# Two fp32r parts of the activations in turn in one row, by stage, with displaced weights and three orders of the products

## The chip, the cores and the metric

The kernel runs on one core of one Trainium2 chip. The metric is the device time of one execution in microseconds. Two executions of the kernel before took 2337.79 and 2339.41 us; their median is 2338.6 us. The profile shown is of one further execution.

## The reference

The program is a two-layer decoder trunk over 272 tokens (16 learned prefix tokens and 256 inputs) of width 2048, with 16 heads of 128 and a squared-ReLU MLP of width 8192. Everything is float32. Layer 0 uses attention with a forget gate, layer 1 uses stick-breaking attention whose keys and values come from a separate projection of the stream:

```
for layer in range(DEPTH):                        # DEPTH = 2
    a = rms_norm(h, norm_attn[layer])
    if layer < N_A_LAYERS:
        proj = a @ fox_w_in[i]                    # q, k, v and the forget gate
        ...
        h = h + o.reshape(b, length, D_MODEL) @ fox_w_o[i]
    else:
        c = rms_norm(h, kv_norm)
        k_s, v_s = jnp.split(c @ w_kv, 2, axis=-1)
        q = split_heads(a @ sb_w_q[i])
        o = stick_breaking_attention(q, shared_k, shared_v)
        h = h + o.reshape(b, length, D_MODEL) @ sb_w_o[i]
    h = h + squared_relu_mlp(rms_norm(h, norm_mlp[layer]), w_up[layer], w_down[layer])
return rms_norm(h, final_norm)[:, N_META:]
```

## The kernel before

Activations lie feature-major: 128 features on the partitions, 16 chunks of features, and the tokens along the row. A matrix product of the model is made of groups (`gemm_group`). A group gives 512 output columns, as four PSUM accumulators (m = 0 to 3) of 128 columns each, over all 16 chunks of the contraction. There are 96 groups, numbered u = 1 to 96 in program order:

- 1 to 12: q, k, v of layer 0 from the activations `a0`, in turn with the attention;
- 13 to 16: output projection of layer 0, from `o0`;
- 17 to 48: MLP of layer 0, four rounds f of four "up" groups (from `m0`) and four "down" groups (from `u0_f`);
- 49 to 52: queries of layer 1 (from `a1`); 53 to 60: keys and values (from `kv`), in turn with the attention; 61 to 64: output projection (from `o1`);
- 65 to 96: MLP of layer 1, as before with `m1` and `u1_f`.

Layer 0, keys and values use all 272 tokens (t0 = 0); the rest of layer 1 uses 256 (t0 = 16).

Precision is kept by splitting. Every float32 operand is held as two fp32r parts: a rounded part, hi, which ScalarE (ACT) writes, and the rest, lo, which VectorE (DVE) writes by a subtraction. One chunk of one accumulator then takes three products with one pass each: weights hi with activations hi, weights hi with activations lo, and weights lo with activations hi. A group is 4 x 16 x 3 = 192 products, and the 96 groups are 18,432 (line L175). Each product carries its own load of 128 x 128 weights.

A weight block of two chunks is loaded by a DMA on SP's queue into a `raw` tile (4 buffers), split by ACT (L215, `whi`) and DVE (L216, `wlo`) into tiles of a pool of 4 buffers each, and used by 24 products. Each tile has rows of 576 elements, of which 512 are used, from element 0 on for 272 tokens and from element 16 on for 256.

The activations of a stage lie in a tile of class `Split`, 16 chunks at 640 elements each. Hi and lo are two contiguous stretches of that row: for 272 tokens at elements 48 and 368, for 256 tokens at elements 0 and 320. TensorE reads 272 or 256 elements in one piece for each product. `split_chunk`, `put_split` and the end of an up group in `mlp` write these parts.

The order of a group's products is fixed on TensorE by added dependencies (`gemm_matmul`). The three products of a chunk come one after the other for 272 tokens, and all products of one kind of a run come before the next kind for 256 tokens. The order of ACT's and DVE's work is set by a scheduler when the program is built.

Of the kernel before, what the change touches and what calls it, by code (L numbers as in the profile page):

```python
# [9 lines left out]
F32 = mybir.dt.float32  # L10
F32R = mybir.dt.float32r
AF = mybir.ActivationFunctionType
ALU = mybir.AluOpType
AX = mybir.AxisListType

P = 128
D = 2048
NC = D // P
M = 16
# [4 lines left out]
QSCALE = 1.0 / math.sqrt(P)  # L24
N_FF = 4

ROWS = {0: (48, 368), M: (0, 320)}
XROW = 640

G_A0, G_M0, G_KV, G_A1, G_M1, G_FIN = range(6)  # L30
# [3 lines left out]
def yoco_kernel(ctx: ExitStack, tc: tile.TileContext, hT_in, gains, b_f, w_f, w_qkv0, w_o0, w_up, w_dn,  # L34
                w_kv, w_q1, w_o1, outT):
    nc = tc.nc
# [5 lines left out]
    wspl = ctx.enter_context(tc.tile_pool(name="wspl", bufs=4))  # L42
# [9 lines left out]
    hT = const.tile([P, NC, T], F32, name="hT")  # L52
# [65 lines left out]
    class Split:  # L118


        def __init__(self, label, t0):
            n = T - t0
            self.t0 = t0
            rows = xs.tile([P, NC * XROW + 64], F32R, tag="x", name=f"x_{label}")
            hi, lo = ROWS[t0]
            rows = rows[:, hi:hi + NC * XROW].rearrange("p (c t) -> p c t", c=NC)
            d = lo - hi
            self.hi, self.lo = rows[:, :, :n], rows[:, :, d:d + n]

    def split_chunk(sp, gi, c):  # L130

        g = g_sb[:, gi, c:c + 1]
        nc.scalar.activation(sp.hi[:, c], hT[:, c, sp.t0:], AF.Copy, scale=g)
        nc.vector.scalar_tensor_tensor(out=sp.lo[:, c], in0=hT[:, c, sp.t0:], scalar=g,
                                       in1=sp.hi[:, c].bitcast(F32), op0=ALU.mult, op1=ALU.subtract)

    class Norm:

# [42 lines left out]
    def gemm_group(wblk, sp, t0, evac, before={}, after={}, load_x=None):  # L181

        uid[0] += 1
        u = uid[0]
        accs = [pacc.tile([P, 512], F32, tag="acc", name=f"acc_{u}_{m}") for m in range(4)]
        n = T - t0
        for kb in range(4):
            src_w = wblk[kb].rearrange("p (k c) -> p k c", k=4)  # L190
            if kb in before:
                before[kb]()
            piece = 1 if load_x is not None and kb < 2 else 2
            raws = [wraw.tile([P, 2, 512], F32, tag="raw", name=f"raw_{u}_{kb}_{hf}") for hf in range(2)]
            for k0 in range(0, 4, piece):
                if load_x is not None:
                    load_x(range(4 * kb + k0, 4 * kb + k0 + piece))
                if load_x is not None and kb == k0 == 0:

                    for c0 in (0, 256):  # L200
                        nc.scalar.dma_start(raws[0][:, 0, c0:c0 + 256], src_w[:, 0, c0:c0 + 256])
                else:
                    nc.sync.dma_start(raws[k0 // 2][:, k0 % 2:k0 % 2 + piece], src_w[:, k0:k0 + piece])
            parts = []
            for hf in range(2):
                whi, wlo = (wspl.tile([P, 2, 576], F32R, tag=f"w{x}", name=f"w{x}_{u}_{kb}_{hf}") for x in ("hi", "lo"))
                o = 16 if t0 else 0
                whi, wlo = whi[:, :, o:o + 512], wlo[:, :, o:o + 512]
                boxes = [(o, piece, 0, 512) for o in range(0, 2, piece)]
                if load_x is not None and kb == hf == 0:  # L210
                    boxes[:1] = [(0, 1, 0, 256), (0, 1, 256, 512)]
                for o, no, c0, c1 in boxes:
                    src = raws[hf][:, o:o + no, c0:c1]
                    hp, lp = whi[:, o:o + no, c0:c1], wlo[:, o:o + no, c0:c1]
                    on_act = nc.scalar.activation(hp, src, AF.Copy)  # L215
                    on_dve = nc.vector.tensor_tensor(out=lp, in0=src, in1=hp.bitcast(F32), op=ALU.subtract)  # L216
                parts.append((whi, wlo))
            if kb in after:
                with tc.issue_after(on_act.ins), tc.issue_after(on_dve.ins):
                    after[kb]()  # L220

            if load_x is not None and kb == 0:
                runs = [([kc], range(4)) for kc in range(4)]
            elif kb in (0, 3):
                runs = [(range(4), [m]) for m in range(4)]
            else:
                runs = [(range(2 * hf, 2 * hf + 2), range(4)) for hf in range(2)]
            pinned[0] = load_x is None
            for kcs, ms in runs:
                pairs = ((0, sp.hi), (0, sp.lo), (1, sp.hi))  # L230
                if t0:
                    products = [(kc, m, *pair) for pair in pairs for kc in kcs for m in ms]
                else:
                    products = [(kc, m, *pair) for m in ms for kc in kcs for pair in pairs]
                left = {m: 3 * len(kcs) for m in ms}
                for kc, m, part, x in products:
                    first, left[m] = kb == kc == 0 and left[m] == 3 * len(kcs), left[m] - 1
                    gemm_matmul(accs[m][:, :n], parts[kc // 2][part][:, kc % 2, m * P:(m + 1) * P], x[:, 4 * kb + kc],
                                start=first, stop=kb == kc == 3 and left[m] == 0)
                if kb == 3:  # L240
                    for m in ms:
                        evac(m, accs[m][:, :n])

    def residual_add(c, acc, t0):
        nc.vector.tensor_tensor(out=hT[:, c, t0:], in0=acc, in1=hT[:, c, t0:], op=ALU.add)  # L245
# [91 lines left out]
        return t  # L337

    def put_split(sp, h, nh, t, n, src):
        hi, lo = (x[:, h:h + nh, t - sp.t0:t - sp.t0 + n] for x in (sp.hi, sp.lo))  # L340
        nc.scalar.activation(hi, src, AF.Copy)
        nc.vector.tensor_tensor(out=lo, in0=src, in1=hi.bitcast(F32), op=ALU.subtract)

    ao = Split("o0", 0)
    for g in range(4):
# [37 lines left out]
        for j in range(4):  # L383
            h = 4 * g + j
# [4 lines left out]
            for i, (o, n) in enumerate(((0, 144), (144, T))):  # L389
                nc.vector.tensor_tensor_reduce(out=s[:, j, o:o + n], in0=ps[:, o:o + n], in1=s[:, j, o:o + n],  # L390
                                               scale=1.0, scalar=3.0e38, op0=ALU.add, op1=ALU.min,
# [4 lines left out]
            for i, (o, n) in enumerate(((0, 144), (144, T))):  # L396
# [7 lines left out]
                                       scalar=fqm_sb[:, g:g + 1], in1=maskM, op0=ALU.subtract, op1=ALU.add)  # L404
        nc.vector.tensor_tensor_reduce(out=s0, in0=ps[:64, :P], in1=s0, scale=1.0,
                                       scalar=3.0e38, op0=ALU.add, op1=ALU.min, accum_out=st[:64, 0:1])
# [6 lines left out]
        for pr in range(2):  # L413
            pp_sb = att.tile([P, 2, 416], F32, tag="pp", bufs=3, name=f"pp_sb_{g}_{pr}")
            for i in range(2):
# [14 lines left out]
                                in0=pm[:, P - M:P].unsqueeze(1).to_broadcast([P, 8, M]))  # L430
# [37 lines left out]
    def mlp(layer, xm, norm, t0, last_evac):  # L468
        box = {}

        def get_rstd():
            box["r"] = norm.finish()

        for f in range(N_FF):
            u = Split(f"u{layer}_{f}", t0)
            for g in range(4):
                def evac(m, acc, g=g):
                    c = 4 * g + m
                    r = tmp.tile([P, T], F32, tag="relu", name=f"relu_{layer}_{f}_{c}")
                    u2 = tmp.tile([P, T], F32, tag="u2", name=f"u2_{layer}_{f}_{c}")  # L480
                    nc.vector.scalar_tensor_tensor(out=r[:, t0:], in0=acc, scalar=0.0, in1=box["r"][:, t0:],
                                                   op0=ALU.max, op1=ALU.mult)
                    nc.scalar.activation(u2[:, t0:], r[:, t0:], AF.Square)
                    nc.scalar.activation(u.hi[:, c], u2[:, t0:], AF.Copy)
                    nc.vector.tensor_tensor(out=u.lo[:, c], in0=u2[:, t0:], in1=u.hi[:, c].bitcast(F32),
                                            op=ALU.subtract)
                gemm_group(w_up[layer, f, g], xm, t0, evac, {2: get_rstd} if f == g == 0 else {})
            for g in range(4):
                def evac(m, acc, g=g):
                    residual_add(4 * g + m, acc, t0)  # L490
                    if f == N_FF - 1:
                        last_evac(4 * g + m)
                gemm_group(w_dn[layer, f, g], u, t0, evac)
# [33 lines left out]
    for g in range(4):  # L527
# [30 lines left out]
        for pr in range(2):  # L558
# [3 lines left out]
            for i in range(2):  # L562
# [4 lines left out]
                                    in1=maskB[:, 0:256].unsqueeze(1).to_broadcast([P, 2, 256]))  # L567
            nc.vector.tensor_tensor(out=zp[:, :, 256:400], in0=pb[:, :, :144], op=ALU.add,
                                    in1=maskB[:, 256:400].unsqueeze(1).to_broadcast([P, 2, 144]))
# [15 lines left out]
            for t in (240, 384):  # L585
                nc.vector.tensor_tensor(out=zp[:, :, t:t + M], in0=zp[:, :, t:t + M],
                                        in1=sc[:, 2 * pr:2 * pr + 2, :], op=ALU.add)
# [47 lines left out]
    a, y, t, rs = (fin[:, i, :] for i in range(4))  # L635
# [18 lines left out]
    for c, n in [(12, 1), (13, 1), (14, 1), (15, 1), (0, 2), (2, 2), (4, 2), (6, 2)]:  # L654
        if n == 1:
            nc.vector.scalar_tensor_tensor(out=ob[:, c, :S], in0=hT[:, c, M:], scalar=g_sb[:, G_FIN, c:c + 1],
                                           in1=prs[0], op0=ALU.mult, op1=ALU.mult)
        else:
            nc.vector.tensor_tensor(out=ob[:, c:c + n, :S], in0=hT[:, c:c + n, M:], op=ALU.mult,  # L659
                                    in1=prs[0].unsqueeze(1).to_broadcast([P, n, S]))  # L660
        nc.sync.dma_start(outT[:, c:c + n, :], ob[:, c:c + n, :S])
    for c in (8, 10):
        nc.gpsimd.tensor_tensor(out=ob[:, c:c + 2, :S], in0=hT[:, c:c + 2, M:], op=ALU.mult,
                                in1=pr_sb.unsqueeze(1).to_broadcast([P, 2, S]))
# [52 lines left out]
```

## Time and profile before

| | before |
|---|---|
| median of two executions | 2338.6 us |
| profiled execution | 2337.68 us, span of its instructions 2335.9 us |
| TensorE, matmuls | 2325.1 us busy (100%), 19,030 instructions |
| TensorE, weight loads | 2312.5 us busy (99%) |
| DVE / ACT | 1291.4 us (55%) / 1041.1 us (45%) |
| DMA | 412.32 MB, mean 177 GB/s |
| granted TensorE clock | 0.998 |

Matmuls are pipelined: each lasts some 280 ns in the trace while the next starts after some 120 ns, so 100% busy does not say that TensorE works at its peak. What counts is the pace, the time from the start of one product to the start of the next. It comes out of a window of the trace: its length divided by the number of products in it.

### The profile page before, as it was taken

To read this page: it belongs to the slowest core of one execution; us is meant where nothing else is said; L and a number is where in the kernel's file an instruction comes from. 1 tells how busy PE (TensorE), PEld (TensorE's weight loads), DVE (VectorE), ACT (ScalarE), POOL (GpSimd) and SP (SyncE) were. 2 spreads that over 40 slices of the span, in tenths; PEclk is the share of its full clock that TensorE was granted. 3 is DMA by queue.
4 is the path that set the end of the run, shared out by engine and by line. 5 is a ranking of instruction groups with operands and counts; after the bars stand their busy time and mean duration, and the time that the engine had idled before them with its cause. 6 is when DMAs were issued, how large, how long until landed. Compare 5 with 4: busy or idle time off the path is not lost.

```text
span 2335.9 us, 44808 instructions
## 1 busy us (share of the span) xinstructions
PE 2325.1 (100%) x19030; PEld 2312.5 (99%) x19030; DVE 1291.4 (55%) x1764; ACT 1041.1 (45%) x1397; POOL 39.7 (2%) x58
## 2 busy tenths in 40 slices
PE   9999999999999999999999999999999999999998
PEld 9999999999999999999999999999999999999998
DVE  7666556554455455455665555566555555555554
ACT  6434345443343344344444444445434444443553
POOL 1000000000000000000000000000000000000000
PEclk9999999999999999999999999999999999999999
DMA  7544545555555555555555444455565655656553
GB/s 237 167 160 158 181 154 164 185 177 179 180 171 184 172 186 175 181 173 185 171 190 184 156 145 147 148 184 192 180 193 177 198 183 179 197 182 191 180 190 127
DMA packets 116648, 412.32 MB, mean 177 GB/s; under 512 B 13264, under 2 KB 16736, under 8 KB 116448
## 3 DMA queue, kind: packets, MB, share of 16 engines
q1 hardware_dynamic: 114560, 406.29, 53.6%
q8 instruction: 149, 2.44, 0.5%
q10 hardware_dynamic: 1888, 3.16, 0.4%
q14 instruction: 51, 0.42, 0.1%
HBM read 407.29 MB, written 2.11 MB: 175 GB/s over the span
## 4 chain that ended last, share of the span: by engine, by line
PE 99%; DMA 1%; DVE 0%; ACT 0%; issue 0%; SPq 0%; DVEq 0%; ACTq 0%
PE acc L175 95%; DMA hT<-hT_in 1%; PE ps L387 0%; PE pza L564 0%; PE pv L320 0%; PE po L449 0%; PE po L603 0%; PE po L604 0%; PE pzb L565 0%; PE po L450 0%; PE po L605 0%; DVE ob L659 0%; PE pf L287 0%; PE pf L286 0%; PE pta L579 0%; PE pta L580 0%
## 5 line engine op out<-in xcount | busy, mean ns | idle before, releaser
L216 DVE TENSOR_TENSOR wlo<-raw,whi 128x1024 fp32r<-128x1024 f32 (+1 forms) x773 | 928.1, 1217 | 770.7 <-ACT whi L215 769.3
L215 ACT ACTIVATE whi<-raw 128x1024 fp32r<-128x1024 f32 (+1 forms) x773 | 795.8, 1049 | 1023.6 <-PE acc L175 1003.1
L175 PE MATMUL acc<-x_u,whi 128*128 128x272 f32 (+1 forms) x4096 | 651.9, 284 | 0.0
L175 PE MATMUL acc<-x_m,whi 128*128 128x272 f32 (+1 forms) x4096 | 651.7, 284 | 0.0
L175 PEld LDWEIGHTS acc<-x_m,whi 128*128 128x128 f32 x4096 | 573.7, 189 | 0.1
L175 PEld LDWEIGHTS acc<-x_u,whi 128*128 128x128 f32 x4096 | 573.8, 189 | 0.0
L175 PE MATMUL acc<-x_u,wlo 128*128 128x272 f32 (+1 forms) x2048 | 445.3, 284 | 0.0
L175 PE MATMUL acc<-x_m,wlo 128*128 128x272 f32 (+1 forms) x2048 | 445.2, 284 | 0.0
L175 PE MATMUL acc<-x_a,whi 128*128 128x272 f32 (+1 forms) x2048 | 362.2, 289 | 0.1
L175 PEld LDWEIGHTS acc<-x_u,wlo 128*128 128x128 f32 x2048 | 327.6, 189 | 0.0
L175 PEld LDWEIGHTS acc<-x_m,wlo 128*128 128x128 f32 x2048 | 327.5, 189 | 0.0
L175 PEld LDWEIGHTS acc<-x_a,whi 128*128 128x128 f32 x2048 | 303.7, 189 | 2.1 <-issue 0.7
L175 PE MATMUL acc<-x_a,wlo 128*128 128x272 f32 (+1 forms) x1024 | 255.0, 287 | 0.0
L175 PE MATMUL acc<-x_kv,whi 128*128 128x272 f32 x1024 | 194.1, 288 | 0.0
L175 PEld LDWEIGHTS acc<-x_a,wlo 128*128 128x128 f32 x1024 | 176.7, 189 | 0.9 <-issue 0.5
L175 PE MATMUL acc<-x_o,whi 128*128 128x272 f32 (+1 forms) x1024 | 162.2, 282 | 0.0
L175 PEld LDWEIGHTS acc<-x_kv,whi 128*128 128x128 f32 x1024 | 160.6, 188 | 0.4
L175 PE MATMUL acc<-x_kv,wlo 128*128 128x272 f32 x512 | 147.3, 288 | 0.0
L175 PEld LDWEIGHTS acc<-x_o,whi 128*128 128x128 f32 x1024 | 141.9, 188 | 0.1
L245 DVE TENSOR_TENSOR hT<-acc,hT 128x272 f32<-128x272 f32 (+1 forms) x160 | 69.1, 432 | 88.1 <-PE acc L175 86.8
L175 PE MATMUL acc<-x_o,wlo 128*128 128x272 f32 (+1 forms) x512 | 110.5, 282 | 0.0
L175 PEld LDWEIGHTS acc<-x_kv,wlo 128*128 128x128 f32 x512 | 96.5, 188 | 0.1
(221 smaller groups left out, 972.2 us busy)
## 6 DMA issues: line engine op xcount, KB each, us to landing
raw<-w_up SPq DMA_DIRECT2D x256, 512.0 KB, 4.4
raw<-w_dn SPq DMA_DIRECT2D x256, 512.0 KB, 4.4
raw<-w_qkv SPq DMA_DIRECT2D x92, 512.0 KB, 3.8
raw<-w_o SPq DMA_DIRECT2D x64, 512.0 KB, 4.1
raw<-w_kv SPq DMA_DIRECT2D x64, 512.0 KB, 3.8
raw<-w_q SPq DMA_DIRECT2D x32, 512.0 KB, 4.6
fk<-f_dram ACTq DMA_DIRECT2D x4, 544.0 KB, 5.2
raw<-w_qkv SPq DMA_DIRECT2D x7, 256.0 KB, 4.4
```

Source lines behind the costliest of these rows:

```text
L175: ins = nc.tensor.matmul(*args, **kw).ins
L215: on_act = nc.scalar.activation(hp, src, AF.Copy)
L216: on_dve = nc.vector.tensor_tensor(out=lp, in0=src, in1=hp.bitcast(F32), op=ALU.subtract)
L245: nc.vector.tensor_tensor(out=hT[:, c, t0:], in0=acc, in1=hT[:, c, t0:], op=ALU.add)
```

## The change

The same products are computed. Changed are where the parts lie and, in some stages, the order of the products.

Activations: a table by stage says how hi and lo share a row. A unit of 0 keeps two stretches (`a0`, `kv`, `u0_1`, at elements 48 and 368 as before). Any other unit puts hi and lo in turn, in pieces of that many elements: 16 (64 bytes) for `o0`, `m0`, `u0_0`, `u0_3`, `a1` and `m1`; 8 (32 bytes) for `u0_2` and `u1_3`; 32 for `o1` and `u1_0`; 64 for `u1_1`; 128 (512 bytes) for `u1_2`. A product then reads its part in pieces of one unit with gaps of one unit. ACT and DVE write the parts in the same pieces.

Weights: hi and lo of a block share one tile of rows of 1088 elements, hi in 512 elements and lo in the next 512, starting at element o. Function `way(u)` gives o, by the group's place g = 0 to 3 in its stage: 0 for groups 1 to 12 and 53 to 60, 16g (64 bytes a step) elsewhere, and in the down groups of layer 1 16 times g // 2. In the up groups of round f = 3 of both layers the elements of hi and lo alternate, so that a weight load steps by two elements.

Order of the products: ABC (the three of a chunk in turn), BAC (weights hi with activations lo first) or SERIES (kind by kind). Up groups use ABC, BAC, SERIES, ABC in rounds f = 0 to 3. Down groups of layer 1 alternate ABC and SERIES. All others use ABC; so `a1` and `o1` go from SERIES to ABC.

```
+ROWS = {"a0": (0, 48), "kv": (0, 48), "o0": (16, 0), "m0": (16, 0), "u0_0": (16, 0), "u0_1": (0, 48), "u0_2": (8, 0),
+        "u0_3": (16, 0), "a1": (16, 0), "o1": (32, 0), "m1": (16, 0), "u1_0": (32, 0), "u1_1": (64, 0),
+        "u1_2": (128, 0), "u1_3": (8, 0)}
+ABC, BAC, SERIES = range(3)
+def way(u):
+    if u <= 12 or 53 <= u <= 60:
+        return 0, 0, ABC
+    f, g = divmod((u - 17) % 48, 8) if 17 <= u <= 48 or u >= 65 else (0, (u - 1) % 4)
+    if 5 <= u <= 16 or u in (49, 50, 51, 52, 61, 62, 63, 64):
+        return 0, 16 * g, ABC
+    if g < 4:
+        return f == 3, 16 * g, (ABC, BAC, SERIES, ABC)[f]
+    g -= 4
+    if u < 49:
+        return 0, 16 * g, ABC
+    return 0, 16 * (g // 2), (ABC, SERIES)[g % 2]
...
-            hi, lo = ROWS[t0]
-            rows = rows[:, hi:hi + NC * XROW].rearrange("p (c t) -> p c t", c=NC)
-            d = lo - hi
-            self.hi, self.lo = rows[:, :, :n], rows[:, :, d:d + n]
+            self.unit, o = ROWS[label]
+            rows = rows[:, o:o + NC * XROW].rearrange("p (c t) -> p c t", c=NC)
+            if self.unit:
+                rows = rows[:, :, :2 * n].rearrange("p c (l i t) -> p c l i t", i=2, t=self.unit)
+                self.hi, self.lo = rows[:, :, :, 0], rows[:, :, :, 1]
+            else:
+                self.unit = 16
+                self.hi, self.lo = lines(rows[:, :, :n], 16), lines(rows[:, :, 320:320 + n], 16)
...
-                whi, wlo = (wspl.tile([P, 2, 576], F32R, tag=f"w{x}", name=f"w{x}_{u}_{kb}_{hf}") for x in ("hi", "lo"))
-                o = 16 if t0 else 0
-                whi, wlo = whi[:, :, o:o + 512], wlo[:, :, o:o + 512]
+                apart, o, order = way(u)
+                both = wspl.tile([P, 2, 1088], F32R, tag="w", name=f"w_{u}_{kb}_{hf}")[:, :, o:o + 1024]
+                if apart:
+                    both = both.rearrange("p k (t i) -> p k i t", i=2)
+                    whi, wlo = both[:, :, 0], both[:, :, 1]
+                else:
+                    whi, wlo = both[:, :, :512], both[:, :, 512:]
...
-                if t0:
+                if order == BAC:
+                    pairs = pairs[1], pairs[0], pairs[2]
+                if order == SERIES:
                     products = [(kc, m, *pair) for pair in pairs for kc in kcs for m in ms]
```

`split_chunk`, `put_split` and the end of an up group in `mlp` read and write the same numbers of elements as before, through views cut into pieces of a unit (`lines`).

More of the change, by code (lines that the diff above doesn't have):

```diff
@@ L25, with lines @@
 N_FF = 4
-ROWS = {0: (48, 368), M: (0, 320)}
+ROWS = {"a0": (0, 48), "kv": (0, 48), "o0": (16, 0), "m0": (16, 0), "u0_0": (16, 0), "u0_1": (0, 48), "u0_2": (8, 0),
[14 more added lines that the diff above has]
+    return 0, 16 * (g // 2), (ABC, SERIES)[g % 2]
+def lines(x, unit):
+    return x.rearrange("p c (l t) -> p c l t", t=unit)
 XROW = 640
@@ L124, in __init__ @@
             rows = xs.tile([P, NC * XROW + 64], F32R, tag="x", name=f"x_{label}")
-            hi, lo = ROWS[t0]
-            rows = rows[:, hi:hi + NC * XROW].rearrange("p (c t) -> p c t", c=NC)
-            d = lo - hi
-            self.hi, self.lo = rows[:, :, :n], rows[:, :, d:d + n]
+            self.unit, o = ROWS[label]
[6 more added lines that the diff above has]
+                self.hi, self.lo = lines(rows[:, :, :n], 16), lines(rows[:, :, 320:320 + n], 16)
     def split_chunk(sp, gi, c):
         g = g_sb[:, gi, c:c + 1]
-        nc.scalar.activation(sp.hi[:, c], hT[:, c, sp.t0:], AF.Copy, scale=g)
-        nc.vector.scalar_tensor_tensor(out=sp.lo[:, c], in0=hT[:, c, sp.t0:], scalar=g,
-                                       in1=sp.hi[:, c].bitcast(F32), op0=ALU.mult, op1=ALU.subtract)
+        src = lines(hT[:, c:c + 1, sp.t0:], sp.unit)
+        nc.scalar.activation(sp.hi[:, c:c + 1], src, AF.Copy, scale=g)
+        nc.vector.scalar_tensor_tensor(out=sp.lo[:, c:c + 1], in0=src, scalar=g,
+                                       in1=sp.hi[:, c:c + 1].bitcast(F32), op0=ALU.mult, op1=ALU.subtract)
     class Norm:
@@ L339, in put_split @@
     def put_split(sp, h, nh, t, n, src):
-        hi, lo = (x[:, h:h + nh, t - sp.t0:t - sp.t0 + n] for x in (sp.hi, sp.lo))
+        l0 = (t - sp.t0) // sp.unit
+        hi, lo = (x[:, h:h + nh, l0:l0 + n // sp.unit] for x in (sp.hi, sp.lo))
+        src = lines(src, sp.unit)
         nc.scalar.activation(hi, src, AF.Copy)
@@ L483, in evac @@
                     nc.scalar.activation(u2[:, t0:], r[:, t0:], AF.Square)
-                    nc.scalar.activation(u.hi[:, c], u2[:, t0:], AF.Copy)
-                    nc.vector.tensor_tensor(out=u.lo[:, c], in0=u2[:, t0:], in1=u.hi[:, c].bitcast(F32),
+                    src = u2[:, t0:].rearrange("p (c l t) -> p c l t", c=1, t=u.unit)
+                    nc.scalar.activation(u.hi[:, c:c + 1], src, AF.Copy)
+                    nc.vector.tensor_tensor(out=u.lo[:, c:c + 1], in0=src, in1=u.hi[:, c:c + 1].bitcast(F32),
                                             op=ALU.subtract)
```

## The prediction

> **What bounds the kernel now.** I read the page first, then TensorE's waits, then windows of the stages.
>
> ```profile
> span 2335.9 us, 44808 instructions
> ...
> PE 2325.1 (100%) x19030; PEld 2312.5 (99%) x19030; DVE 1291.4 (55%) x1764; ACT 1041.1 (45%) x1397; POOL 39.7 (2%) x58
> ...
> PE 99%; DMA 1%; DVE 0%; ACT 0%; issue 0%; SPq 0%; DVEq 0%; ACTq 0%
> PE acc L175 95%; DMA hT<-hT_in 1%; PE ps L387 0%; PE pza L564 0%; PE pv L320 0%; PE po L449 0%; PE po L603 0%; PE po L604 0%; PE pzb L565 0%; PE po L450 0%; PE po L605 0%; DVE ob L659 0%; PE pf L287 0%; PE pf L286 0%; PE pta L579 0%; PE pta L580 0%
> ```
>
> The chain that ended last is TensorE for 99%, the products of line L175 for 95%. Its waits, in us in total, times, longest:
>
> ```profile
> PE pr_fin L648 <- DVE fin L642: 1.3, 1, 1.3
> PE idle L61 <- DVE mean_w L57: 1.1, 1, 1.1
> PE pms_fin L616 <- ACT sq_fin L628: 0.3, 1, 0.3
> ```
>
> That is 2.7 us in all, so only the pace of 18,432 products counts. One ns on each is 18.4 us, and a change of 2% (some 47 us, about what a measurement of this kernel can tell from no change) is 2.5 ns. Windows: the MLP of layer 0 without its first 20 ns, the last three groups of `o1`, and 30 groups of the MLP of layer 1; the count includes two or three products open at the edges.
>
> ```profile
> 429.80:1187.90 758.10, 758.10 (x6148) 758.02 (x6147) 396.83 (x484) 326.81 (x419) 0.00 (x0) 1.00 0.55 178
> 1532.80:1598.00 65.20, 65.20 (x578) 65.20 (x577) 42.55 (x60) 33.89 (x49) 0.00 (x0) 1.00 0.61 194
> 1620.80:2299.20 678.40, 678.40 (x5762) 678.40 (x5761) 363.96 (x432) 302.55 (x385) 0.00 (x0) 1.00 0.58 187
> ```
>
> These hold 32, 3 and 30 groups of 192 products, so the paces are 758.1/6144 = 123.4 ns at 272 tokens and 65.2/576 = 113.2 or 678.4/5760 = 117.8 ns at 256 tokens. The last two differ though code, form and layout are the same. Within one group of `m1`, before and after the two matmuls of the norm that interrupt it, it flips:
>
> ```profile
> 1598.10:1608.90 10.80, 10.80 (x98) 1.00 0.52 158
> 1609.80:1620.60 10.80, 10.80 (x94) 1.00 0.65 213
> ```
>
> Less some 2.5 open at the edges that is 113 and 118 ns. Both stretches use the same addresses modulo 256 bytes. So at 256 tokens there are two stable phases of weight loads against rows, 4.6 ns apart, and a break chooses between them.
>
> How far is that from the stream itself? Mean ns of one by form:
>
> ```profile
> L175 PE MATMUL acc<-x_m,whi 128*128 128x272 f32 x2048 | 379.3, 287 | 0.0
> L175 PE MATMUL acc<-x_m,whi 128*128 128x256 f32 x2048 | 272.4, 281 | 0.0
> L387 PE MATMUL ps<-kT,qT 128*128 128x272 f32 x32 | 9.9, 393 | 0.0
> L387 PE MATMUL ps<-kT,qT 128*128 128x144 f32 x32 | 6.5, 285 | 0.0
> L286 PE MATMUL pf<-x_a,wf 128*32 128x272 f32 x16 | 4.1, 286 | 0.0
> L579 PE MATMUL pta<-eh,ntri_r 128*128 128x512 f32 x8 | 3.2, 395 | 0.0
> L581 PE MATMUL pta<-eh,nones_r 128*128 128x288 f32 x8 | 2.4, 296 | 0.0
> ```
>
> Plain float32 matmuls (L387) take (393 - 285)/128 = 0.84 ns a column. An fp32r product at 272 takes about half a float32 one's share, so I put its stream at 0.42 ns a column: 114 ns for 272, 107 for 256. Above the stream stand 9.7 ns at 272, and 6.2 or 10.8 ns at 256. The gate products (L286) load only 32 columns of weights and last as long as the others, 286 against 287 ns: the excess at 272 hangs on reading the row.
>
> **The change part by part.** The profiled execution took 2337.7 us, 1.8 beyond its span and 0.9 under the median. I sum against 2337.7.
>
> *Unchanged.* Groups 1 to 12, 53 to 60 and group 29 (`u0_1`, g = 0) keep layout, displacement modulo 256 bytes and order: 21 of 96, no cost. Transfers keep sizes and queues.
>
> *Units of 16 and 8.* At 272 tokens these are 32 groups (6144 products): `o0` 4, `m0` 16, `u0_0`, `u0_2`, `u0_3` 4 each. At 256 they are 24 groups (4608): `a1` 4, `m1` 16, `u1_3` 4. No row shows fp32r rows read in such small pieces. The nearest are L579 and L581, two pieces each. From 272 to 288 columns the stream explains 6.7 of 296 - 287 = 9 ns, leaving 2.3 ns for one break, if all of it is the break's. From 272 to 512 it explains 101 of 108 ns, leaving 7 ns for 240 columns and one break; in proportion, the excess of 272 alone would be 9.7 x 240/272 = 8.6 ns, leaving nothing for the break. So a break costs 0 to 2.3 ns. I take nothing for the break itself, by the longer row, but let the excess grow with the stretch of row that is walked. A half-used stretch doubles the 128-byte pieces touched: 8.5 more at 272, 8 more at 256. The excess per piece is 6.2/8 = 0.8 to 10.8/8 = 1.35 ns. I take 0.8, since part of the excess will belong to each product, not to its length. That is 6.8 ns x 6144 = 42 us and 6.4 ns x 4608 = 29 us. The lower end is below nothing, as a new phase can gain (second rival).
>
> [...]
>
> *Units of 32, 64 and 128* (`o1`, `u1_0`, `u1_1`, `u1_2`, 16 groups): whole 128-byte pieces, as many as before: 0. At 2.3 ns a break (7, 3 and 1) it would be 16, 7 and 2 ns a product.
>
> *Displacement.* Before, every pair of weights and row starts 64 bytes apart modulo 256. Now 53 groups differ (10,176 products). The size of a changed meeting of the two streams is the flip's 4.6 ns, either way: 47 us up or down at most. As interleaved rows meet several displacements at once, I take 0.
>
> *Orders.* 192 products and 192 loads a group remain, and the flip happens within one order. I take 0, inside the same bound.
>
> *Alternating weights* (8 groups, 1536 products).
>
> ```profile
> L175 PEld LDWEIGHTS acc<-x_m,whi 128*128 128x128 f32 x4096 | 573.7, 189 | 0.1
> L286 PEld LDWEIGHTS pf<-x_a,wf 128*32 128x32 f32 x16 | 1.7, 108 | 0.2
> ```
>
> A load takes (189 - 108)/96 = 0.84 ns a column, 108 ns for 128. It is hidden under a pace of 118 to 123 ns, with 10 to 15 ns to spare. A step of two elements costs nothing while it fits there. If the load takes twice as long, the pace becomes 216 plus the 5 ns that separate 108 from 113.2, thus 221: 768 x (221 - 123.4) + 768 x (221 - 117.8) = 154 us. I take 0, because rows already pass through at twice a load's bytes per ns.
>
> *ACT and DVE.* They write the same elements, in pieces.
>
> ```profile
> L216 DVE TENSOR_TENSOR wlo<-raw,whi 128x1024 fp32r<-128x1024 f32 x764 | 922.3, 1224 | 769.9 <-ACT whi L215 768.5
> L215 ACT ACTIVATE whi<-raw 128x1024 fp32r<-128x1024 f32 x764 | 790.6, 1055 | 1021.5 <-PE acc L175 1003.1 <-ACT sq_m L150 6.4 <-DMA fqm_sb<-f_dram 5.1
> ```
>
> Eight blocks a group cost DVE 9.8 and ACT 8.4 us of a group's 22.6 to 23.7; TensorE covers them. Doubled, DVE's 52% in the first window becomes 94%, still under. Hi and lo in one tile mean that ACT's next hi part waits for the last reader of lo as well. In SERIES that is 8 products, 0.9 us; the block is due three blocks (72 products, 8.5 us) later and takes 1.06 + 1.22 us. With that cover gone each late block would stall TensorE by its excess. I take 0.
>
> Sum: 2337.7 + 42 + 29 = 2409 us.
>
> **The rivals.**
>
> *The layout does not matter.* For it: paces are constant over thousands of products while ACT, DVE and DMA work beside them, and the 512-column row shows no break. Against it: the flip. The phases at 256 may settle otherwise; all 36 slow groups at 113.2 would give 36 x 192 x 4.6 = 32 us less. So 2338, between 2305 and 2365.
>
> *Faster.* The interleaved row takes weights and rows apart at the start of each product. The groups at 256 then stay at 113.2 (32 us less), and half of the 9.7 ns goes in the 35 changed groups at 272: 6720 x 4.85 = 33 us. That is 2273. It decides once the products at 272 gain 2.3 ns besides all groups at 256. For it: the flip shows 4.6 ns to be had with the same code. Against it: at 272 no second pace appears in 6144 products. [...]
>
> *Far slower.* Either each break costs 2.3 ns: 16 breaks a product at 272 and unit 16 are 37 ns, over all stages 2.3 x (5376 x 16 + 768 x 33 + 3840 x 15 + 1536 x 7 + 768 x 35) = 475 us, 2813 us. Or alternating weights double the load: 2409 + 154 = 2563 us. For it: L581. Against it: L579.
>
> **How the numbers follow.** Forecast 0.43, its own range 2365 to 2465 (0.5 to 1.35 ns a piece and part of the displacement). No effect 0.29, faster 0.14, far slower 0.14. The range 2275 to 2565 leaves out about half of each outer rival. Slower by over 2% are the far slower rival and nearly all of the forecast, 0.54; within 2% the first rival and the forecast's lower end, 0.32; faster 0.14.
>
> **What would show it.** Right: in windows, groups 17 to 24 and 41 to 48 near 130 ns and the first rounds of `m1` near 120 to 124; `u1_1` and `u1_2` within 113 to 118; group 29 at 123.4. The weight load of round 3 longer than 189 ns, but its pace no worse than that of round 0. Wrong: one pace for all units (first rival), paces under 120 at 272 (second), a pace that falls with 8, 16, 32, 64, 128 as the breaks do, or 221 ns in round 3 (third). A wait of TensorE for ACT or DVE of over 10 us in all would break the cover that I assume.

## The result, and the profile after

The changed kernel takes 2389.36 us (2389.03 and 2389.70) against 2338.6 us: a ratio of 1.022, 95% interval 1.0203 to 1.0237, slower by 50.8 us. The forecast was slower, 2409 us, with 2275 to 2565.

The page of the changed kernel, the same parts as before:

```profile
span 2387.2 us, 44824 instructions
...
PE 2376.2 (100%) x19030; PEld 2364.0 (99%) x19030; DVE 1289.7 (54%) x1764; ACT 1042.4 (44%) x1397; POOL 35.7 (1%) x58
...
PE 99%; DVE 0%; ACT 0%; issue 0%; DVEq 0%; ACTq 0%
```

TensorE's waits are the three of before, 2.7 us in all:

```profile
PE pr_fin L689 <- DVE fin L683: 1.3, 1, 1.3
PE idle L88 <- DVE mean_w L84: 1.1, 1, 1.1
PE pms_fin L657 <- ACT sq_fin L669: 0.3, 1, 0.3
```

So nothing new is waited for, and the granted clock is 0.998 as before. The span grew by 51.3 us and TensorE's busy time by 51.1: the products follow each other more slowly. Windows of the changed kernel, each of whole groups: `u0_0`, group 29, `u0_2`, the last three of `o1`, the up groups of round 1 in layer 1, `u1_1` in two halves, and three groups of `u1_3`:

```profile
532.49:631.27 98.78, 98.78 (x770) 1.00 0.51 171
729.84:754.16 24.32, 24.32 (x195) 1.00 0.53 174
924.47:1021.06 96.59, 96.59 (x770) 1.00 0.53 175
1566.40:1635.73 69.33, 69.33 (x578) 1.00 0.55 183
1820.80:1913.41 92.61, 92.61 (x770) 1.00 0.55 183
1913.41:1959.48 46.07, 46.07 (x386) 1.00 0.57 183
1959.48:2004.71 45.23, 45.23 (x386) 1.00 0.56 185
2283.06:2351.08 68.02, 68.02 (x578) 1.00 0.57 186
```

Each length is divided by 192 products a group (the count in brackets includes two or three open at the edges); paces are in ns:

| groups | row | pace before, ns | pace after, ns |
|---|---|---|---|
| `u0_0` (21 to 24) | unit 16, 272 tokens | 123.4 | 98.78/768 = 128.6 |
| group 29 of `u0_1` | two stretches, displacement as before | 123.4 | 24.32/192 = 126.7 |
| `u0_2` (37 to 40) | unit 8 | 123.4 | 96.59/768 = 125.8 |
| `o1` (62 to 64) | unit 32, 256 tokens | 113.2 | 69.33/576 = 120.4 |
| `m1`, round 1 (73 to 76) | unit 16 | 117.8 | 92.61/768 = 120.6 |
| `u1_1` (77, 78), weights at 0 | unit 64 | 117.8 | 46.07/384 = 120.0 |
| `u1_1` (79, 80), weights at 64 bytes | unit 64 | 117.8 | 45.23/384 = 117.8 |
| `u1_3` (93 to 95) | unit 8 | 117.8 | 68.02/576 = 118.1 |

Three things are not as forecast. Unit 8 costs less than unit 16, though it cuts the row twice as often and walks through the same stretch. The place of the weights moves the pace in rows of unit 64. And group 29, of which nothing was changed, went from 123.4 to 126.7 ns.

### The profile page after: what moved, and what is told of

Read it like the earlier page. It is cut to its first block, busy times and chain, and to the rows that moved or that the text cites. A ratio compares the mean times of both kernels' runs of the same rounds, so it can differ in the third digit from the quotient of the medians.

```text
span 2387.2 us, 44824 instructions
## 1 busy us (share of the span) xinstructions
PE 2376.2 (100%) x19030; PEld 2364.0 (99%) x19030; DVE 1289.7 (54%) x1764; ACT 1042.4 (44%) x1397; POOL 35.7 (1%) x58
## 4 chain that ended last, share of the span: by engine, by line
PE 99%; DVE 0%; ACT 0%; issue 0%; DVEq 0%; ACTq 0%
PE acc L207 96%; PE ps L427 0%; PE pza L605 0%; PE pv L358 0%; PE po L489 0%; PE po L644 0%; PE idle L88 0%; PE po L645 0%; PE pzb L606 0%; PE po L490 0%; PE po L646 0%; DVE ob L700 0%; PE pf L325 0%; PE pf L324 0%; PE pta L620 0%; PE pta L621 0%
## 5 line engine op out<-in xcount | busy, mean ns | idle before, releaser
L252 DVE TENSOR_TENSOR w<-raw,w 128x1024 fp32r<-128x1024 f32 (+1 forms) x773 | 929.2, 1217 | 859.3 <-ACT w L251 857.6
L251 ACT ACTIVATE w<-raw 128x1024 fp32r<-128x1024 f32 (+1 forms) x773 | 803.8, 1058 | 1099.5 <-PE acc L207 1081.0
L207 PE MATMUL acc<-x_m,w 128*128 128x272 f32 (+1 forms) x6144 | 767.4, 288 | 0.0
L207 PEld LDWEIGHTS acc<-x_m,w 128*128 128x128 f32 x6144 | 766.2, 190 | 0.1
L207 PE MATMUL acc<-x_u,w 128*128 128x272 f32 (+1 forms) x6144 | 758.2, 286 | 0.0
L207 PEld LDWEIGHTS acc<-x_u,w 128*128 128x128 f32 x6144 | 757.1, 189 | 0.0
L207 PE MATMUL acc<-x_a,w 128*128 128x272 f32 (+1 forms) x3072 | 395.5, 289 | 0.0
L207 PEld LDWEIGHTS acc<-x_a,w 128*128 128x128 f32 x3072 | 383.7, 189 | 2.7 <-issue 1.1
L207 PE MATMUL acc<-x_kv,w 128*128 128x272 f32 x1536 | 196.8, 288 | 0.0
L207 PE MATMUL acc<-x_o,w 128*128 128x272 f32 (+1 forms) x1536 | 193.5, 288 | 0.0
```

Source lines behind the costliest of these rows:

```text
L207: ins = nc.tensor.matmul(*args, **kw).ins
```

## The experiments

Two theories stood against each other. Theory A is the forecast's: the cost lies in the interleaved rows and grows with the stretch walked. Theory B: the pace is set by where the stream of a weight load meets the stream of a row, that is by the distance between their starts modulo 256 bytes (the displacement), and the meeting locks into a phase (one of several steady paces at the same addresses) that an unbroken stream carries on. All paces below are a window's length over its products. Each run but the last is one execution, beside one of the kernel before. A code cut shows added and removed lines; `...` stands for lines left out. Lines that name `layer1` or `changed` are edits of the changed kernel; `changed(u)` is its `way(u)`.

### Nothing but the shared weight tile

```
+ROWS = {k: (0, 48) for k in ("a0", "kv", "o0", "m0", "u0_0", "u0_1", "u0_2", "u0_3")}
+ROWS.update({k: (0, 0) for k in ("a1", "o1", "m1", "u1_0", "u1_1", "u1_2", "u1_3")})
...
+    layer1 = 49 <= u <= 52 or u >= 61
+    return 0, 16 * layer1, SERIES if layer1 else ABC
```

> Edit: the changed kernel with rows, displacements and orders set back to those of before, so that only the shared weight tile and the cut views remain. Theory A (the cost lies in the interleaved rows): 2338 us, 123.3 ns a product at 272 tokens in the MLP, 113.3 in the last three groups of o1, 117.8 in the MLP at 256. Theory B (the meeting of the weight stream with the row stream sets the pace): the same, since every start keeps its place modulo 256 bytes. Rival C (hi and lo of the weights in one tile change the meeting): group 29 went from 123.3 to 126.7 ns with the same rows, order and displacement, so all MLP groups at 272 would show 126.7 ns, 20 us more.

Measured: 2336.3 us beside 2338.1. Windows of groups 18 to 48, 62 to 64 and 66 to 95:

```profile
453.29:1187.37 734.08, 734.08 (x5955) 1.00 0.55 178
1532.18:1597.46 65.28, 65.28 (x578) 1.00 0.60 193
1620.08:2298.48 678.40, 678.40 (x5762) 1.00 0.57 187
```

These are 123.3, 113.3 and 117.8 ns, the paces of before. The shared tile and the cut views cost nothing, and rival C falls.

### The rows alone

```
+    layer1 = 49 <= u <= 52 or u >= 61
+    return 0, 16 * layer1, SERIES if layer1 else ABC
```

> Edit: only the rows of the changed kernel (hi and lo in turn by the table), weights at 0 and 16 and the orders of before. Theory A: nearly the whole difference, 2380 to 2390 us, with 128.9 ns in the groups at 272 that read units of 16. Theory B: less than the whole, 2360 to 2375 us, because a part belongs to displacements in contiguous rows; the units of 64 and 128 at 256 tokens give 117.8 ns as before, since they had 117.8 at displacement 16 in the changed kernel, and 8 gives 117 to 118.

Measured: 2390.1 us, 52.1 more than 2338.1. Windows of `u0_0`, `u0_2`, the last three groups of `o1`, `m1` in round 1, `u1_1`, `u1_3`:

```profile
532.96:631.95 98.99, 98.99 (x771) 1.00 0.52 171
924.65:1020.93 96.28, 96.28 (x770) 1.00 0.54 175
1567.86:1636.98 69.12, 69.12 (x578) 1.00 0.56 183
1822.70:1915.82 93.12, 93.12 (x771) 1.00 0.56 182
1915.82:2006.27 90.45, 90.45 (x770) 1.00 0.58 187
2282.96:2351.45 68.49, 68.49 (x579) 1.00 0.56 185
```

Paces: 128.9 for unit 16 and 125.4 for unit 8 at 272 tokens; 120.0 for unit 32, 121.3 for 16, 117.8 for 64 and 118.9 for 8 at 256. The rows alone cost as much as the whole change. In time that is theory A's number and not theory B's; in the order of the units it is neither the stretch (8 and 16 walk the same) nor the breaks (8 has twice as many). Theory B had the 117.8 ns of unit 64 right, but not the 117 to 118 ns of unit 8.

### The displaced weights alone

```
+    layer1 = 49 <= u <= 52 or u >= 61
+    return 0, changed(u)[1], SERIES if layer1 else ABC
```

> Edit: only the displaced weights (16g elements, in the down groups of layer 1 16 times g // 2; no alternating weights), rows and orders of before. Theory A: 2338 us, paces as before. Theory B: paces move with g in contiguous rows: at 256 tokens 120.0 ns at displacement 0 and 117.8 at 16 (as units 64 and 128 showed), at 272 some groups near 126.7; 10 to 25 us more than before.

The rows are set back as in the first run. Measured: 2362.5 us, 24.4 more. Windows of groups 21, 22, 24 (weights at 0, 64 and 192 bytes, 272 tokens), 73 and 75 (at 0 and 128 bytes, 256 tokens):

```profile
527.95:551.63 23.68, 23.68 (x194) 1.00 0.57 179
551.63:575.95 24.32, 24.32 (x194) 1.00 0.55 173
600.27:624.33 24.06, 24.06 (x194) 1.00 0.55 175
1800.25:1823.28 23.03, 23.03 (x194) 1.00 0.56 185
1845.90:1868.69 22.79, 22.79 (x195) 1.00 0.57 186
```

That is 123.3, 126.7 and 125.3 ns, then 120.0 and 118.7, in contiguous rows and with the same order. Theory A expected no effect; theory B holds here: a shift of the weights alone moves the pace, by 2.0 to 3.4 ns a product at 272 tokens.

The whole change (50.8 us) costs less than rows and displacement apart add up to (52.1 + 24.4). In interleaved rows the displacement, with the order that came along, helps some groups and hurts others: `m1` has 121.3 ns with the weights at 64 bytes throughout, and in the changed kernel 120.0 to 121.1 in rounds 0 and 1 (without group 65, which the norm interrupts) but 121.3 to 122.6 in round 2.

### The orders alone

> Edit: only the orders of the products (ABC, BAC, SERIES by round and stage), rows and displacements of before. Theory A and theory B with both parts of a row at the same place modulo 256: no effect, 2338 us, 123.3 and 117.8 ns whatever the order. Rival (the order carries the phase, as group 29 after the BAC groups suggests): the up groups of rounds 1 and 2 at 272 leave 123.3 ns for about 126.7 and the groups after them stay there, some 10 to 20 us.

```
+    return 0, 16 * layer1, changed(u)[2]
```

Rows and displacements are those of before. Measured: 2336.8 us beside 2338.1; windows of groups 18 to 48 and 66 to 95:

```profile
453.13:1187.21 734.08, 734.08 (x5954) 1.00 0.55 178
1619.93:2298.32 678.39, 678.39 (x5762) 1.00 0.57 187
```

To 0.01 us the lengths of the run with the shared tile alone. Orders do nothing in contiguous rows with the displacement of before, and the rival falls.

### A break ahead of group 29

```
+            if u == 29 and kb == 0:
...
+                for _ in range(4):
+                    gemm_matmul(st[:, :P], mean_w, mean_w, start=True, stop=True)
```

> Edit: the changed kernel with four plain float32 matmuls of 128 columns ahead of group 29, nothing else. Theory B1 (at 272 tokens too there are two stable phases for the same addresses, and an unbroken stream carries the phase on): group 29 falls from 126.7 to 123.3 ns, as it has it alone with the rows of the changed kernel; groups 30 to 32 stay at 126.7, 126.7 and 125.3. Rival (group 29's pace comes from something that only the whole change has): it stays at 126.7. Time 2389 us in both.

Measured: 2389.4 us beside 2337.6. Groups 29 and 30:

```profile
730.60:754.37 23.77, 23.77 (x196) 1.00 0.56 177
754.37:778.69 24.32, 24.32 (x195) 1.00 0.53 174
```

The first window holds the restart after the break; behind its first 24 products the others start 123.3 ns apart. Group 29's 126.7 came over from the groups before it. So at 272 tokens, too, the same addresses have two stable paces.

### Products of 272 columns ahead of those of 256

```
+            if u in (49, 65) and kb == 2:
...
+                for _ in range(16):
+                    gemm_matmul(st[:, :T], parts[0][0][:, 0, :P], parts[0][0][:, 0, 48:48 + T], start=True, stop=True)
```

> Edit: the kernel before, with 16 extra fp32r products of 272 columns (into a PSUM buffer that nobody reads) right after the norm's matmul in groups 49 and 65; the norm's matmul is held in its place by the same added dependency as the products. Theory B1: a product of 272 columns ahead of those of 256 leads into the fast phase, as at the passage from the layer 0 MLP into group 49; groups 49 to 52 and 65 to 95 go from 117.8 to 113.3 ns, 30 us less, 4 us for the extra products: 2312 us. Rival (the pace at 256 tokens belongs to the stage and not to the phase): 2342 us, 117.8 ns kept.

Measured: 2341.6 us beside 2337.6. Groups 66 to 95:

```profile
1624.64:2303.04 678.40, 678.40 (x5763) 1.00 0.58 187
```

The pace stayed at 117.8 ns. A miss: the 16 longer products ahead did not by themselves lead into the fast phase (113.3 ns at 256 tokens).

### A map of the displacement in steps of 16 bytes

```
+    if 17 <= u <= 48 or u >= 65:
+        f, g = divmod((u - 17) % 48, 8)
+        return 0, 4 * (4 * f + g % 4), SERIES if layer1 else ABC
```

> Edit: contiguous rows and the orders of before; in the two MLPs the weights start 16 (4f + g) bytes into their row, so that each of the 16 places of 256 bytes is taken by one up and one down group. Theory B: the pace is a function of the displacement of weights against rows modulo 256 bytes alone, equal for the up and the down group of a place; at 272 tokens 123.3 at 64, 126.7 at 128 and 192, 125.3 at 0; at 256 tokens 120.0, 117.8, 118.7 and 117.8 at 0, 64, 128 and 192; between them steps, if the memory is divided by 64 bytes, or a slope. No place falls under 123.3 or 117.8 unless a phase flips to 113.3. Time 2360 us. Rival (only the displacement modulo 64 bytes counts): four equal rows of values.

Measured: 2354.8 us beside 2337.6. Windows of groups 22 and 30 (weights 16 and 80 bytes into their row, 272 tokens), 68 and 73 (48 and 64 bytes, 256 tokens):

```profile
549.78:574.10 24.32, 24.32 (x195) 1.00 0.51 173
743.06:766.74 23.68, 23.68 (x194) 1.00 0.54 176
1681.40:1704.02 22.62, 22.62 (x195) 1.00 0.55 187
1795.10:1816.87 21.77, 21.77 (x195) 1.00 0.58 191
```

At 272 tokens the 16 places give, from 0 to 240 bytes: 123.3, 126.7, 123.3, 126.7, 126.7, 123.4, 126.7, 126.7, 126.7, 125.7, 125.8, 125.0, 125.4, 125.0, 126.6 and 126.7, the same to 0.1 ns in the up and the down group of a place (but for group 17 at 0, which the norm interrupts). It is a function of the place within 256 bytes with no shorter period, so the rival of 64 bytes falls; it is neither steps of 64 nor a slope, and no place is better than 123.3. The rows stayed where they were, so place and distance to the row are not told apart. At 256 tokens, apart from 64 bytes, it runs from 116.7 (208 and 224 bytes) to 120.0 (112, 160 and 240), not always alike in both groups (118.3 and 120.0 at 144), against the expectation that none but the fast phase lies under 117.8. At 64 bytes, the displacement of before, group 73 came from 48 bytes and ran at 21.77/192 = 113.4, and group 77 came from 112 bytes and ran as fast:

```profile
1885.25:1907.03 21.78, 21.78 (x194) 1.00 0.58 189
```

So 48 bytes is not the only place that leads in. A step from 0 to 64 bytes did not: groups 62, 66 and 74 made it in the run with the displaced weights alone, and all had 117.8 (group 74: 22.62/192).

### Other units

```
+ROWS.update({"u0_0": (4, 0), "u0_1": (2, 0), "u0_2": (34, 0), "u0_3": (136, 0), "u1_0": (4, 0), "u1_1": (2, 0), "u1_2": (1, 0), "u1_3": (8, 0)})
```

> Edit: weights and orders of before, only the rows of the down groups interleaved, by units of 4, 2, 34 and 136 elements (u0_0 to u0_3) and 4, 2, 1 and 8 (u1_0 to u1_3). Theory A1 (the excess grows with the number of breaks in a row): 4 and 2 far above the 125.4 of 8 (130 ns and more), 136 like contiguous rows. [...] Theory B (only which 64-byte stretches meet): units of 4 and 2 like 8 (125 and 118 to 119 ns), as they walk through the stretches in the same way, 34 near 16's 128.9, 136 near 123 to 127.

Measured: 2602.3 us beside 2337.6. Windows of `u0_0`, `u0_1`, `u0_2`, `u0_3`, `u1_0`, the up groups of round 1 in layer 1, `u1_1`, and the up groups of round 2; the up groups' rows are contiguous here:

```profile
525.65:621.22 95.57, 95.57 (x770) 1.00 0.54 177
715.94:902.80 186.86, 186.86 (x770) 1.00 0.27 90
997.54:1099.93 102.39, 102.39 (x770) 1.00 0.50 165
1194.66:1290.24 95.58, 95.58 (x771) 1.00 0.54 177
1790.79:1880.82 90.03, 90.03 (x771) 1.00 0.57 187
1880.82:1967.88 87.06, 87.06 (x770) 1.00 0.60 193
1967.88:2144.49 176.61, 176.61 (x771) 1.00 0.30 96
2144.49:2231.58 87.09, 87.09 (x770) 1.00 0.60 193
```

Unit 4: 124.4 ns, better than 8 (125.4) and 16 (128.9) with two and four times as many breaks: theory A1 falls. At 256 tokens unit 4 has 117.2, a little under the 117.8 of contiguous rows. Unit 2: 243.3 and, at 256 tokens, 230.0, as much as unit 1 (230.0, `u1_2`); theory B had units of 2 at the pace of 8, and falls there. Unit 34 gives 133.3, where theory B expected some 129, and 136 gives 124.5. So pieces of four elements run at 124.4 ns, close to the 123.3 of contiguous rows, and pieces of two take twice the time, 243.3.

The up groups are the finding of this run: 87.06/768 and 87.09/768 = 113.4 ns in groups whose rows, weights and order are those of before, where they had 117.8. Those of round 1 follow unit 4, whose products at 117.2 ns are not slow.

### Into the fast phase by slow products, or by a step from 48 to 64 bytes

```
+            if u in (49, 65) and kb == 2:
...
+                for _ in range(8):
+                    gemm_matmul(st[:, :256], parts[0][0][:, 0, :P], parts[0][0][:, 0, ::2], start=True, stop=True)
```

> Edit: the kernel before, with 8 extra fp32r products that read every second element of 512 (some 230 ns each, by the unit of 1 in e7_units) right after the norm's matmul in groups 49 and 65, written to a PSUM buffer that nobody reads. Theory B2 (the stream enters the fast phase when products that are held up by their rows come ahead, as in e7_units, where the groups after units of 4, 2 and 1 ran at 113.4 to 113.6 ns): groups 49 to 52 and 65 to 95 at 113.3 instead of 117.8, 30 us less and 4 us for the extra products, 2312 us. Rival (the entry in e7_units hung on the whole round before, not on its last products): 117.8 kept, 2342 us.

```
-                o = 16 if t0 else 0
+                o = (12 if u in (49, 65) else 16) if t0 else 0
```

> Edit: the kernel before, with the weights of groups 49 and 65 alone at 48 bytes into their row instead of 64. Theory B3 (a change of the displacement from 48 to 64 bytes leads into the fast phase, as in e6_map, where group 73 at 64 bytes followed groups at 48 and ran at 113.3): groups 49 and 65 at 117.8, groups 50 to 52 and 66 to 95 at 113.3, 29 us less than before, 2309 us. Rival (in e6_map the whole sequence of places led there): 117.8 kept and 2338 us.

Measured: 2310.9 and 2309.4 us beside 2337.7. Groups 66 to 95 of the first; of the second, group 65, its products ahead of the norm's matmul (72 of them), and groups 66 to 95:

```profile
1620.20:2273.00 652.80, 652.80 (x5762) 1.00 0.59 194
```

```profile
1596.31:1619.36 23.05, 23.05 (x197) 1.00 0.56 184
1596.31:1604.79 8.48, 8.48 (x75) 1.00 0.36 129
1619.36:2272.17 652.81, 652.81 (x5763) 1.00 0.59 194
```

652.8/5760 = 113.3 ns against 678.4/5760 = 117.8 before, for the same products at the same addresses. Both ways in work; both rivals fall. Group 65 ran at 8.48/72 = 117.8 as expected; its whole window is longer because the norm's matmul stands in it. Group 49, expected at 117.8, had 123.2 ahead of the norm's matmul and 117.8 behind it. What the ways in have in common stays open: unit 4 led in without slow products, and group 77 of the map from 112 bytes.

### Alternating weights alone

```
+    layer1 = 49 <= u <= 52 or u >= 61
+    return (17 <= u <= 48 or u >= 65) and (u - 17) % 48 // 4 == 6, 16 * layer1, SERIES if layer1 else ABC
```

> Edit: the kernel before with the shared weight tile, and in the up groups of round 3 of both layers hi and lo of the weights alternating by one element (loads step by 8 bytes); rows, displacements at the start of the row and orders of before. Prediction's term (a load has 10 to 15 ns to spare, and two of four elements of each 16 bytes are used): weight loads of 189 ns as elsewhere, 2338 us. Theory B (a load that walks twice the bytes meets the row in other places): 2 to 5 ns more in these 8 groups, 3 to 8 us. Rival of the prediction (a load of double length): 221 ns a product, 150 us more.

The condition holds for the up groups of round 3. Measured: 2342.3 us beside 2337.7, 4.6 more. Windows of groups 41 to 44, 45 to 48 (whose weights do not alternate), 89 to 92 and 93 to 95; then the weight loads within the first window:

```profile
1000.14:1097.42 97.28, 97.28 (x770) 1.00 0.51 174
1097.42:1194.70 97.28, 97.28 (x770) 1.00 0.52 174
2147.51:2239.68 92.17, 92.17 (x770) 1.00 0.56 184
2239.68:2304.96 65.28, 65.28 (x578) 1.00 0.58 193
```

```profile
L196 PEld LDWEIGHTS acc<-x_m,w 128*128 128x128 f32 x768 | 97.3, 196 | 0.0
```

A load lasts 196 ns instead of 189, nowhere near twice the time of its columns, so the far slower rival falls. The pace rises to 126.7 and 120.0 all the same, although by the prediction's estimate of 108 ns a load of 7 ns more, 115, still fits under the pace; why it rises is not shown. The contiguous groups behind take over a phase: a bad one in `u0_3` (126.7), the good one in `u1_3` (113.3), so their shares nearly cancel.

### The better version, timed

> The same kernel as e9_in48, now timed in five rounds. Theory B3: 2309 to 2310 us, a ratio of 0.988 to the kernel before, in every execution, since the entry is set by the program and not by chance. Rival (the phase is settled anew in each execution by small shifts in time): times spread between 2309 and 2338 us.

Measured: 2309.87 us (2309.26 to 2310.90, four runs) against 2337.53 (2336.47 to 2337.86): a ratio of 0.9882, interval 0.9866 to 0.9899. It beats both kernels, by 1.2% the one before, and the narrow spread of these four runs speaks for an entry that the program sets.

## Why the prediction was right or wrong

The direction held, and the first and main step: TensorE alone sets the end, no cover of ACT, DVE or transfers was lost (its waits stayed at 2.7 us), and only the pace counts. The size came out at 50.8 us for a forecast of 71, and that it came so near is in part luck: the term that gave the forecast its size charged a row for each 128-byte piece that it walks through, and the runs show no such rule. Stage by stage, from the spans of the stages in both traces:

- Units of 16 and 8 at 272 tokens: forecast 42, measured 28 us (31 with the rows alone). At 256: forecast 29, measured 14 (15 with the rows alone). The row excess per 128 bytes was the term that was mis-sized, and its reason was wrong: 4, 8 and 16 walk the same stretch and have 124.4, 125.4 and 128.9 ns at 272 tokens, and unit 4 costs nothing at 256 (117.2).
- Units of 32 to 128: forecast 0, measured 8 us, 5 of it in `o1`, which lost the fast phase (113.2 to 120.4; 120.0 by the rows alone). With the weights at their old place units of 64 and 128 are free (117.8), as the forecast had it; units of 32, whole 128-byte pieces too, are not (120.0).
- Displacement: forecast 0 within 47 us either way. Alone it costs 24 us; in `u0_1` of the changed kernel it and the carried phase cost 2.3. The step "the excess at 272 hangs on reading the row" is wrong as far as it excluded the weights.
- Orders: 0, right in contiguous rows. In rows of unit 16 with displaced weights it was not separated.
- Alternating weights: forecast 0; 4.6 us more in the run of its own, 4.3 of it in the eight groups themselves. The reason given (a load has time to spare) holds by its length and does not decide the pace.
- "Unchanged" group 29: forecast 123.4, measured 126.7, by the phase it inherited. The flip within one group of `m1` was read rightly as two phases, but not carried over to 272 tokens.

Of the signs that the prediction named, groups 18 to 24 and 41 to 48 (126.7 to 128.9) and the first rounds of `m1` (120.0 to 121.1) came out near what was named, and a load of round 3 lasted 196 ns. `u1_1` missed (120.0 in two groups of four), and so did group 29; round 3 was no worse than round 0 in layer 0, but was in layer 1 (120.7 to 122.2 against 120.0 to 121.1). One slip of the working changes nothing: above a stream of 114 ns the excess at 272 is 9.4 ns, not 9.7.

Of the rivals, "no effect" fails by the rows' 52 us alone, "far slower" by 196 ns a load and by unit 4. "Faster" was wrong for this change, but its first half was real: 28 us of the fast phase at 256 tokens are to be had, by an entry and not by a layout.

Open: why a place, a unit or an entry gives the pace it gives. The runs show that the interleaved rows alone cost what the whole change costs (52.1 and 50.8 us), that the pace depends on the place within 256 bytes (123.3 to 126.7 ns at 272 tokens), and a memory of what came before (113.3 and 117.8 ns at the same addresses); they give no rule that would have foretold 128.9 for unit 16 or the way into the fast phase. That it is the meeting of the two streams which does this is argued, not shown. In the changed kernel the effects of order and alternation within interleaved rows were not taken apart.

## What to carry to other kernels

Where matrix products stream at full rate, read the pace of one product by window: here a difference of 4.5 ns between stages with the same code (113.3 and 117.8) was a state to be found, and moving the weights of two groups by 16 bytes was worth 1.2%. Judge a layout by more than one entry into it: a group can inherit its pace from the group before it (group 29: 126.7 ns, and 123.3 behind a break), and a long stage did not shed it (30 groups kept 117.8 where 113.3 was to be had). Displacements that were tuned for one layout are not to be added to gains or losses of another layout: here 52 and 24 us gave 51 together.

## What the runs showed of the hardware that was not expected

A stream of fp32r products had two steady paces at the same addresses (113.3 and 117.8 ns at 256 columns, 123.3 and 126.7 at 272); at 256 columns each was kept over 5760 products. The place of the weights within 256 bytes moved the pace at contiguous rows from 123.3 to 126.7 ns at 272 columns. fp32r rows in pieces of four elements ran at nearly the pace of contiguous rows (124.4 and 123.3 ns) and in pieces of two at half of it (243.3 ns), while weight loads that step by two elements lasted only 196 instead of 189 ns.
